# Left sums kept in scratch and built over the operands, and a new order of products in the two-level pairs of a one-core tanh(a @ b + bias)

## The chip, the cores and the metric

The kernel runs on one core of one Trainium2 chip. The metric is the time of one execution on the device in microseconds (us); several executions of the same kernel are timed and their median is given. The engines named below are TensorE (matrix products), VectorE (elementwise sums, transposes), ScalarE (tanh, copies), GpSimd and SyncE (in this kernel both mostly start transfers between DRAM and the core's memory; each works off its own list in order).

## The reference

```
a: 4096 x 4096 float32, b: 4096 x 4096 float32, bias: 4096 float32
out = tanh(a @ b + bias)          # 4096 x 4096 float32
```

## The kernel before, in words

**One level of saving.** The output is worked on in 4 chunks of 1024 columns (`c`), and in each chunk in 16 pairs of two 128-row blocks. Such an item is a 2 x 2 arrangement of blocks: `a11`, `a12`, `a21`, `a22` are the item's four quadrants of a (two row blocks by two halves of the inner dimension; each 128 x 2048 numbers in fp16, already transposed), and `b11` to `b22` are the quadrants of the chunk's b. Instead of eight products of quadrants the kernel computes seven, in the manner of Strassen and Winograd, from sums of quadrants (`PRODUCTS`, L36): m2 = s2 b11, m5 = s5 b22, m3 = a11 d3, m1 = s1 d1, m4 = a22 d4, m6 = s6 e6, m7 = s7 e7. The left sums belong to one item: s2 = a21 - a22, s5 = a12 - a11, s1 = a22 - a11, s6 = a21 - a11, s7 = a22 - a12. The right sums (d1, d3, d4, e6, e7) belong to the chunk. Each of the seven products is 16 matmuls of 128 x 128 by 128 x 512, added up in PSUM (`product` L456, matmul L469); its result is combined with others on VectorE, goes through tanh on ScalarE and is stored (`result` L491, `store` L483, `after` L496). Every sum on VectorE is one `tensor_tensor` (`tt`, L145 and 146).

**Where a quadrant comes from.** In chunk 0 and in the first items of chunk 1 ("natural" items) rows of a are loaded by GpSimd (`load_nat` L226), transposed on VectorE (`turn` L278) and stored once by SyncE into a scratch copy in DRAM (`keep` L298). Later items fetch the four quadrants from scratch on SyncE's queue (`fetch` L303). The quadrants' tiles come two deep (`quads`, bufs=2), the output tiles `o` three deep (`outs`, bufs=3), two small pools (`sums`, bufs=2, and `spare`) hold left sums, and `asum` (L320) makes a left sum from two quadrants: s6 in a21's place and s7 in a12's place, the others in a tile of `sums` or `spare`.

**Order.** The work is laid out by hand in slots, seven per item; `at_slot` (L1431) puts a call into a slot and `prepare` (L1434) places an item's loads, transposes, stores or fetches, and its sums. In each slot the calls are issued in list order, then the products of that slot. Each engine executes its own part of this list in order.

**A second level.** In chunks 1 to 3 two neighbouring items (`p` and `q`) also share products: m3 and m4 of the two (in some pairs m6) are computed together as seven half-size products of eight 256-wide matmuls each instead of two whole ones (`twice` L651, `twice_left` L634 for the left halves `h`, or `twice_four` L923). In chunks 2 and 3, after four and two such items (`FOURS`, L84), the slot list ends and `turn_over` (L1308) leads into a stage of pairs in which four of the seven products are split in this way: `four` (L997), which runs four pairs in chunk 2 and six in chunk 3. In it

- m4, m2, m3 and one or both of m5 and m6 are split. `group0` (L894), `group1` (L900) and `single` (L913) issue the seven half-size products, `multiply` (L874, matmul L885) each one of them; `left` (L848) makes the half-size left sums v1 to v4, each 128 x 1024, in one of four `h` tiles; `copy` and `third` (L889 to L904) move partial results on ScalarE, and the small sums of 128 x 256 join them on VectorE;
- m1 and m7 (and in the last pair of a chunk that is followed by another also m6) stay whole (`whole` L942, matmul L946);
- the right-hand forms t1 to t4 and blocks for m2 and m6 stream in from DRAM on GpSimd's queue (`pull_four` L810, load L816), each as soon as a tile is let go (`let_go` L818, and `hand_back` L829 for tiles that first hold a left sum); those for m3 and m4 stay; those for m5 are made by VectorE in the first pair at the steps given in `M5_AT` (L83, `m5_forms` L972);
- `seed` (L977) zeroes a half of a PSUM bank on ScalarE, `between` (L866) names the half bank for a split product's second partial sum, `four_sum` (L951) makes the left sums, and `give_back` (L980) with `BACK` (L92) fetches the next chunk's operands near the end of chunk 2.

Before, a pair runs m4 beside m2, then m3 beside m6 (or m5), m1 of q, m5 (or m6) with the two halves of m1 of p in between, and m7 of p and q. The last results of a pair are put off into the next one (`left_over`, `more` L992, called four times with an even share).

Of the kernel before, what the change touches and what calls it, by code (L numbers as in the profile page):

```python
# [8 lines left out]
P = 128  # L9
# [72 lines left out]
AHEAD = (), ("a22", "a21", "a11")  # L82
M5_AT = {"t1": -2, "t3": 1, "t2": 3, "t4": 7}  # L83
# [11 lines left out]
    ("b11", 0): 12, ("e6", 0): 2, ("e6", 1): 8, ("m5", "t3"): 13,  # L95
# [10 lines left out]
QUADS = ("a11", "a12", "a21", "a22")  # L106

# [8 lines left out]
def kernel(  # L116
# [203 lines left out]
    def asum(n, name, half=None):  # L320
        s = aset[n]
        x, y = {
            "s2": ("a21", "a22"), "s5": ("a12", "a11"), "s1": ("a22", "a11"),
            "s6": ("a21", "a11"), "s7": ("a22", "a12"),
        }[name]
        over = {"s6": "a21", "s7": "a12"}.get(name)
        if half == 1:
            pass
        elif name == "s6" and n in partner and by_two(n, "m6"):
            s[name] = side[:, :, ds(NB, NB)].rearrange("p a (b m) -> p a b m", m=P)  # L330
            tt(s[name], by_four(s[x]), by_four(s[y]), SUB)
            return
        elif over is None or stays(n):
            s[name] = new_sum([P, T, P], fp16, name, n)
        else:
            s[name] = s[over]
        ts_ = ds(0, T) if half is None else ds(half * TP, TP)
        tt(s[name][:, ts_], s[x][:, ts_], s[y][:, ts_], SUB)
# [295 lines left out]
    def twice_left(n, what, name):  # L634
        left = TWO[what][0]
        p, q = (
            [by_four(aset[i][left])[:, ds(h * TP // TB, TP // TB)] for h in range(2)]
            for i in (n, partner[n])
        )
        x, y = {  # L640
            "s2": (q[0], q[1]), "s5": (p[1], p[0]), "s1": (q[1], p[0]),
            "s6": (q[0], p[0]), "s7": (p[1], q[1]),
        }[name]
        tt(by_four(lefts[PLACE[what][name]]), x, y, SUB)
# [163 lines left out]
    free, held, placed, left_count, homes, wanted, reserved = [], {}, {}, [0], {}, [], []  # L808
# [9 lines left out]
    def let_go(n, what, name):  # L818
        tag = held.pop((what, name))
        c = items[n][0]  # L820
        if wanted and wanted.pop(0):
            reserved.append(tag)
        elif c < NC - 1 and not queue and tag != "sum":
            bring_block(c, tag[:-2], int(tag[-1]))
        else:
            free.append(tag)
        pull_four()

    def hand_back(c):  # L829
        if reserved:  # L830
            tag = reserved.pop(0)
            if c < NC - 1 and tag != "sum":
                bring_block(c, tag[:-2], int(tag[-1]))
            else:
                free.append(tag)
                pull_four()
# [29 lines left out]
    def between(n, what):  # L866
        if n not in fours:
            return bank(n, 0, "w")[:, HALF[TWO[what][3]]]
        i, where, half = {
            "m2": (n, "c", 0), "m4": (n + 1, "c", 1), "m3": (n, "w", 0),  # L870
        }.get(what, (n + 1, "w", 1) if homes.get(what) == "d" else (n, "c", 0))
        return bank(i, 0, where)[:, HALF[half]]

    def multiply(n, what, to, left_, right):  # L874
# [11 lines left out]
        if what in ("m2", "m6"):  # L886
            let_go(n, what, right)
# [63 lines left out]
    def four_sum(n, name, there):  # L951
        x, y = {
            "s2": ("a21", "a22"), "s5": ("a12", "a11"), "s1": ("a22", "a11"),
            "s6": ("a21", "a11"), "s7": ("a22", "a12"),
        }[name]
        st = aset[n]
        if there in QUADS:
            st[name] = st[there]
        elif there in "AB":
            st[name] = side[:, :, ds(NB * "AB".index(there), NB)].rearrange("p a (b m) -> p a b m", m=P)  # L960
        else:
            pool = {"wide": wide, "sum": sums, "spare": spare}.get(there, bops)
            st[name] = pool.tile([P, T, P], fp16, name=name, tag="sum" if there == "spare" else there)
        tt(by_four(st[name]), by_four(st[x]), by_four(st[y]), SUB)

# [26 lines left out]
    def more(calls):  # L992
        for f in left_over[:-(-len(left_over) // calls)]:
            f()
            left_over.pop(0)

    def four(n):  # L997
# [4 lines left out]
        x, y = ("m5", "m6") if last or leave else ("m6", "m5")  # L1002
        mine = {x: "d", y: "w"}
        homes.update(mine)
        pair = {i: items[i][1][0] for i in (p, q)}
        st = {i: state.setdefault((i, 0), {}) for i in (p, q)}
        home = {
            ("s6", p): "a21", ("s6", q): "a21", ("s1", q): "A",
            ("s5", p): "B", ("s1", p): "a11", ("s5", q): "a11", ("s7", p): "a12", ("s7", q): "a12",
        }  # L1010
        if last or leave:
            wanted.extend([1, 0, 1])
        if leave:
            home.update({
                ("s1", p): "A", ("s1", q): "sum",
                ("s6", p): "wide", ("s6", q): "wide", ("s7", p): "wide",
            })

        def make(name, i):
            four_sum(i, name, home[name, i])  # L1020

# [8 lines left out]
        def one_whole(what, i):  # L1030
            _, left_, right = next(v for v in PRODUCTS.values() if v[0] == what)
            whole(i, left_, right, ((bank(i, 0, mine.get(what, "z")), ds(0, NB)),), what in mine)

        def end(name, i, r, j):
            if name == "ds":
                result(st[i][name], pair[i], r, c, j)
            else:
                nc.scalar.activation(st[i][name], st[i][name], TANH)
                store(st[i][name], pair[i], r, c, j)

        def take(what, i, later=False):
            to = bank(i, 0, mine[what])
            if what == "m6":
                tt(st[i]["o"], st[i]["o"], to, ADD)
                ready = ("o", i, 1, 1)
            else:
                tt(st[i]["ds"], st[i]["ds"], to, SUB)
                tt(st[i]["s"], to, st[i]["s"], ADD)
                ready = ("s", i, 0, 1)
            if later:  # L1050
                left_over.append(lambda: end(*ready))
            else:
                end(*ready)
# [5 lines left out]
        def take_d(i):  # L1059
            st[i]["ds"] = temps.tile([P, NB], fp32, name="ds", tag="ds")  # L1060
            tt(st[i]["ds"], bank(i, 0, "d"), bias_bc[:, :NB], ADD)

        def take_z(i):
            st[i]["o"] = new_out()
            tt(st[i]["o"], st[i]["s"], bank(i, 0, "z"), SUB)
# [4 lines left out]
        more(4)  # L1070
        group0(n, "m2")
        left(n, "m2", "v2")
        left(n, "m4", "v3")
        if first:
            make("s6", q)
        more(3)
        step(1)
        w, w2 = group1(n, "m4")
        left(n, "m4", "v4")
        w()  # L1080
        left(n, "m2", "v3")
        if last or leave:
            home["s5", p] = "spare" if reserved[0] == "sum" else reserved[0]
            make("s5", p)
        elif not first:
            make("s6", p)
        more(2)
        u, u2 = group1(n, "m2")
        left(n, "m2", "v4")
        more(1)  # L1090
# [3 lines left out]
        if first:  # L1094
            forms_at(1)
        single(n, "m2", 7)
        u()
        seed(p, "c", 0)
        seed(p, "w", 0)
        seed(q, "w", 1)  # L1100
        left(n, "m3", "v1")
        single(n, "m4", 3, 4)
        step(5)
        u2()
        take_d(p)
        single(n, "m2", 3)
        if last or leave:
            home["s5", q] = "spare" if reserved[1] == "sum" else reserved[1]
            make("s5", q)
        elif not first:  # L1110
            make("s6", q)
        step(6)
        seed(p, "d", 0)
        forms_at(2)
        left(n, x, "v1")
        take_d(q)
        group0(n, "m3")
        left(n, "m3", "v2")
        single(n, "m2", 4)
        step(7)  # L1120
        forms_at(3)
        group0(n, x)
        step(8)
        left(n, x, "v2")
        left(n, "m3", "v3")
        forms_at(4)
        for i in (p, q):
            tt(st[i]["ds"], st[i]["ds"], bank(i, 0, "z"), ADD)
        w, w2 = group1(n, "m3")
        step(9)  # L1130
        left(n, "m3", "v4")
        w()
        left(n, x, "v3")
        for i in (p, q):
            result(st[i]["ds"], pair[i], 1, c, 0)
        if not leave:
            make("s1", q)
            forms_at(5)
            seed(p, "w", 0)
        u, u2 = group1(n, x)  # L1140
        left(n, x, "v4")
        forms_at(6)
        hand_back(c)
        if leave:
            make("s1", p)
        single(n, "m3", 7)
        w2()
        if leave:
            make("s6", p)
            fetch(m, "a21")  # L1150
            make("s7", p)
            fetch(m, "a22")
            fetch(m, "a11")
            fetch(m, "a12")
        single(n, x, 7)
        single(n, "m3", 3, 4)
        step(11)
        if leave:
            one_whole("m1", p)
# [749 lines left out]
```

## Time and profile before

| | |
|---|---|
| median of 3 runs | 1522.07 us (1521.95 to 1522.07) |
| span of the one profiled execution | 1520.0 us, that is 2.07 below the median; no other time of that execution is given |
| bytes moved | 384.58 MB, mean 253 GB/s |
| transfers of a<-scratch (SyncE) | 140 of 512 KB, median 5.4 us from issue to landing |
| transfers of out_dram<-o (SyncE) | 222 of 256 KB, 5.1 us |
| loads of form<-form_m (GpSimd) | 133 of 512 KB, 6.5 us |

The span runs from the first to the last instruction of the core. The profile gives for each engine its busy time and its share of the span; TensorE's weight loads (PEld) run beside its matmuls. A row of the timeline reads: start in us, busy us, engine, line, operation, written<-read tiles, their sizes, how many alike in a row, and in brackets the idle time before with what ended it. Tiles carry the names of the program: `a` is a quadrant or a sum in its place, `s` a left sum (or, at 128 x 512, a partial result), `h` a half-size left sum, `ps` a PSUM bank, `ds` a partial result, `o` an output tile, `form` a right-hand form. A row of the view of stretches reads: start and end, length, then busy us (and instructions) of TensorE, weight loads, VectorE, ScalarE and GpSimd, the granted TensorE clock, the busy share of the DMA engines and GB/s. A row of the transfers reads: queue, written<-read, how many, first to last issue, and under it the time from issue to landing. The time of a fetched transfer counts from its issue in its queue, so a wait for another transfer ahead of it lies before the issue.

### The profile page before, as it was taken

What the parts mean: (1) busy time and instruction counts of PE and PEld (TensorE: products, weight loads), DVE (VectorE), ACT (ScalarE), POOL (GpSimd) and SP (SyncE); (2) the same over time, 40 slices, a digit from 0 to 9 for tenths busy, and PEclk for the clock granted to TensorE, in tenths of its full rate; (3) what the DMA queues carried; (4) which work ended last, traced back from release to release, by engine and by line L of the source; (5) the groups of instructions that cost most, each with busy time, mean ns of one, the idle gap of its engine ahead of it and who ended that gap; (6) DMA issues with size and microseconds to landing.
All of it is one profiled execution on the core that took longest, in us unless ns stands there. A gap on an engine that the chain in (4) does not pass through costs nothing.

```text
span 1520.0 us, 23293 instructions
## 1 busy us (share of the span) xinstructions
PE 1514.8 (100%) x8805; PEld 860.0 (57%) x8805; DVE 1213.7 (80%) x1617; ACT 357.8 (24%) x760; POOL 479.2 (32%) x868
## 2 busy tenths in 40 slices
PE   9999999999999999999999999999999999999999
PEld 4444444444445566544444557777744457777776
DVE  6789877777987777677798777888769969888887
ACT  4432111111221122111122212222212312223222
POOL 8775543333603231344460222111122211111110
PEclk9999999999999999999999999999999999999999
DMA  9999998999979998999995889888966789888874
GB/s 186 180 211 258 280 239 217 225 215 229 190 212 292 267 280 269 231 260 237 228 187 159 292 280 318 307 296 315 320 234 195 226 269 341 317 307 303 304 286 160
DMA packets 203029, 384.58 MB, mean 253 GB/s; under 512 B 25122, under 2 KB 100130, under 8 KB 202916
## 3 DMA queue, kind: packets, MB, share of 16 engines
q0 software_dynamic: 117232, 198.50, 56.4%
q1 hardware_dynamic: 85012, 184.26, 34.9%
q8 instruction: 69, 1.13, 0.3%
q10 hardware_dynamic: 672, 0.33, 0.1%
q14 instruction: 44, 0.36, 0.1%
HBM read 329.78 MB, written 138.94 MB: 308 GB/s over the span
## 4 chain that ended last, share of the span: by engine, by line
PE 99%; DVE 0%; DMA 0%; POOL 0%; issue 0%; ACT 0%; POOLq 0%; DVEq 0%
PE ps L469 58%; PE ps L885 22%; PE ps L946 10%; PE ps L1539 5%; PE ps L667 4%; DMA side<-in_b_dram 0%; DVE h L146 0%; DVE a L146 0%; POOL side L1628 0%; POOL first L1608 0%; DVE form L146 0%; DVE o L146 0%; POOL ident L1615 0%; ACT ds L1266 0%; POOLq L1615 0%
## 5 line engine op out<-in xcount | busy, mean ns | idle before, releaser
L469 PEld LDWEIGHTS <-s 128*128 128x128 f16 x2160 | 211.4, 98 | 249.1 <-DVE s L146 0.2
L469 PEld LDWEIGHTS <-a 128*128 128x128 f16 x1920 | 187.9, 98 | 223.3
L469 PE MATMUL ps<-b,s 128*128 128x512 f16 x1148 | 262.0, 379 | 0.0
L469 PE MATMUL ps<-e,a 128*128 128x512 f16 x908 | 206.9, 379 | 0.0
L469 PE MATMUL ps<-d,a 128*128 128x512 f16 x896 | 202.5, 379 | 0.0
L146 DVE TENSOR_TENSOR s<-a,a 128x2048 f16<-128x2048 f16 (+1 forms) x148 | 178.2, 1207 | 12.7 <-DMA a<-scratch 11.5
L885 PEld LDWEIGHTS <-h 128*128 128x128 f16 x1760 | 171.9, 98 | 26.3 <-DVE h L146 0.4
L271 DVE STREAM_TRANSPOSE a<-nat 128x1024 f16<-128x1024 f16 (+2 forms) x202 | 175.2, 912 | 9.8 <-PE ps L469 8.3
L816 POOL DMA_DIRECT2D form<-form_m x133 | 70.7, 532 | 347.3 <-PE ps L885 318.2
L469 PE MATMUL ps<-d,s 128*128 128x512 f16 x656 | 148.3, 379 | 0.0
L146 DVE TENSOR_TENSOR a<-a,a 128x2048 f16<-128x2048 f16 x120 | 146.0, 1217 | 0.0
L243 POOL DMA_DIRECT2D nat<-in_a_dram x176 | 93.4, 535 | 132.9 <-DVE a L271 58.2
L372 POOL DMA_DIRECT2D b<-in_b_dram x192 | 103.8, 546 | 83.7 <-DVE a L271 31.0
L885 PE MATMUL ps<-form,h 128*128 128x256 f16 x768 | 99.4, 273 | 0.1
L146 DVE TENSOR_TENSOR ps<-ps,x 128x256 f32<-128x256 f32 x128 | 54.0, 429 | 56.4 <-ACT x L891 46.1
L885 PEld LDWEIGHTS <-a 128*128 128x128 f16 x904 | 88.5, 98 | 16.6
L493 ACT ACTIVATE o<-ps 128x512 f32<-128x512 f32 x90 | 54.0, 600 | 158.6 <-issue 94.4
L946 PEld LDWEIGHTS <-a 128*128 128x128 f16 x464 | 44.8, 98 | 44.6
L946 PE MATMUL ps<-e,a 128*128 128x512 f16 (+2 forms) x320 | 68.8, 368 | 0.0
L567 ACT ACTIVATE o<-o 128x512 f32<-128x512 f32 x37 | 23.3, 630 | 175.0 <-DVE o L146 175.0
L146 DVE TENSOR_TENSOR ds<-ds,ps 128x512 f32<-128x512 f32 x75 | 50.2, 683 | 13.6 <-PE ps L946 9.3
L146 DVE TENSOR_TENSOR o<-ds,ps 128x512 f32<-128x512 f32 x40 | 27.4, 685 | 41.2 <-issue 28.9
(190 smaller groups left out, 2001.0 us busy)
## 6 DMA issues: line engine op xcount, KB each, us to landing
a<-scratch SPq DMA_DIRECT2D x140, 512.0 KB, 5.4
form<-form_m POOLq DMA_DIRECT2D x133, 512.0 KB, 6.5
out_dram<-o SPq DMA_DIRECT2D x222, 256.0 KB, 5.1
nat<-in_a_dram POOLq DMA_DIRECT2D x288, 128.0 KB, 7.2
scratch<-a SPq DMA_DIRECT2D x48, 512.0 KB, 6.7
b<-in_b_dram POOLq DMA_DIRECT2D x160, 128.0 KB, 5.5
scratch<-a SPq DMA_DIRECT2D x32, 256.0 KB, 5.7
cast<-in_b_dram POOLq DMA_DIRECT2D x64, 128.0 KB, 9.2
```

The lines of the kernel that those rows point to most:

```text
L146: nc.vector.tensor_tensor(out=out_, in0=in0, in1=in1, op=op)
L243: nc.gpsimd.dma_start(out=tl[ds(q * QP, QP), :, :], in_=src.rearrange("(mb p) k -> p mb k", p=QP),)
L271: nc.vector.transpose(dst[:, ds(b0 * tb, n * tb), :].rearrange("P (b t) (mb p) -> P mb b t p", t=tb, p=QP), src[:, :, ds(b0, n), :].rearra ...
L372: nc.gpsimd.dma_start(out=dst[ds(q * QP, QP), ds(t, nt)], in_=src)
L469: nc.tensor.matmul(st[where], at, bt, start=(what == "m2" or n < LEAD and what == "m1") and i == 0, stop=i == len(ts_) - 1, skip_group_che ...
L493: nc.scalar.activation(o, src, TANH)
L567: nc.scalar.activation(o, o, TANH)
L667: nc.tensor.matmul(to, at, bt, start=False, stop=t == TP - 1, skip_group_check=True)
L816: nc.gpsimd.dma_start(out=rights[what, name], in_=forms[what, name])
L885: nc.tensor.matmul(to, at, bt, start=False, stop=t == TP - 1, skip_group_check=True)
L946: nc.tensor.matmul(to[:, half], at[:, t // TB, t % TB], bop[right, t // TB][:, t % TB, half], start=anew and t == 0, stop=t == T - 1, skip ...
L1539: nc.tensor.matmul(mb[m % 4, j], aq[m, kt // T][:, kt % T, :], right(kt, j), start=fresh and kt == k0, stop=stop and kt == k1 - 1, skip_gr ...
```

## The change: what it does

- `asum` follows a table `SUMS`. s2 is made over a21 and s5 over a12. Natural items make them and then store them, so that scratch holds s2 and s5 in the places of a21 and a12; a11 and a22 are still stored right after their transpose. An item that fetches from scratch gets s2 and s5 ready-made and makes neither. s6 is s2 + s1 and s7 is s1 - s5; in the two-level stage s1 is made over a11. s6 moves by two slots and s7 by one in some items. `twice_left` takes its halves by a table.
- `four_sum`, `hand_back` and the lists around it go. A tile of a form is let go by the product that used it, without further holding.
- `four` runs in a new order: m4 beside m3, m2 beside m5, m1 of p, m6 split (or whole, in the pair that leaves a chunk) with m1 of q among it, and m7 of p and q. So m5 is split in all pairs, and m2's and m5's results of both items are finished next to each other. `between` names other half banks. `left_over` holds one call, run at once in the next pair. Seeds, fetches and sums are placed anew around it.
- `turn_over` has fetches, sums and seeds in new places, and fetches a12 of the stage's first two items there, right behind the m7 of p and of q; `after` (L563 and L564) has started a fetch of the same quadrant with each of these m7.
- The constants `M5_AT`, `AHEAD` and `BACK` change with it.

The built program has 8805 matmuls before and after, 1365 two-input operations on VectorE before and 1279 after, 514 and 518 transfers by SyncE.

```diff
-AHEAD = (), ("a22", "a21", "a11")
-M5_AT = {"t1": -2, "t3": 1, "t2": 3, "t4": 7}
+AHEAD = (), ("a21", "a11")
+M5_AT = {"t1": -2, "t3": 1, "t2": 2, "t4": 3}
...
-    ("b11", 0): 12, ("e6", 0): 2, ("e6", 1): 8, ("m5", "t3"): 13,
+    ("b11", 0): 6, ("e6", 0): 2, ("e6", 1): 10, ("m5", "t3"): 12,
...
+SUMS = {
+    "s2": ("a21", "a22", SUB), "s5": ("a12", "a11", SUB), "s1": ("a22", "a11", SUB),
+    "s6": ("s2", "s1", ADD), "s7": ("s1", "s5", SUB),
+}
...
     def asum(n, name, half=None):
         s = aset[n]
-        x, y = {...}[name]
-        over = {"s6": "a21", "s7": "a12"}.get(name)
+        over = {"s2": "a21", "s5": "a12", "s6": "a21", "s7": "a12"}.get(name)
+        if name == "s1" and n in fours:
+            over = "a11"
+        if name in ("s2", "s5"):
+            s[name] = s[over]
+            if not natural(n):
+                return
...
+        x, y, op = SUMS[name]
...
-        tt(s[name][:, ts_], s[x][:, ts_], s[y][:, ts_], SUB)
+        tt(s[name][:, ts_], s[x][:, ts_], s[y][:, ts_], op)
...
     def between(n, what):
...
-            "m2": (n, "c", 0), "m4": (n + 1, "c", 1), "m3": (n, "w", 0),
-        }.get(what, (n + 1, "w", 1) if homes.get(what) == "d" else (n, "c", 0))
+            "m4": (n, "w", 0), "m3": (n + 1, "w", 0), "m2": (n, "w", 1), "m5": (n + 1, "w", 1),
+            "m6": (n, "c", 0),
+        }[what]
...
     def four(n):            # the new order, its main line (not the leaving or last pair)
         step(0)
         group0(n, "m4")
         left(n, "m4", "v2")
-        more(4)
-        group0(n, "m2")
-        left(n, "m2", "v2")
+        more()
+        group0(n, "m3")
+        left(n, "m3", "v2")
         left(n, "m4", "v3")
...
+        u, u2 = group1(n, "m3")
         step(2)
         single(n, "m4", 7)
         w2()
+        left(n, "m3", "v4")
         u()
+        single(n, "m3", 7)
+        u2()
+        forms_at(1)
...
         single(n, "m4", 3, 4)
         step(5)
+        for i in (p, q):
+            asum(i, "s2")
+            asum(i, "s5")
+        left(n, "m2", "v1")
+        take_d(p)
+        seed(p, "d", 0)
+        single(n, "m3", 3)
+        take_d(q)
+        left(n, "m5", "v1")
+        forms_at(2)
+        group0(n, "m2")
+        left(n, "m2", "v2")
+        take_c(p)
+        single(n, "m3", 4)
+        step(6)
+        left(n, "m5", "v2")
+        take_c(q)
+        seed(p, "c", 0)
+        group0(n, "m5")
+        step(7)
+        left(n, "m2", "v3")
+        forms_at(3)
+        w, w2 = group1(n, "m2")
+        left(n, "m5", "v3")
+        w()
+        asum(p, "s1")
+        if not last:
+            fetch(m, "a22")
+        left(n, "m2", "v4")
+        u, u2 = group1(n, "m5")
+        step(8)
+        single(n, "m2", 7)
+        forms_at(4)
+        w2()
+        left(n, "m5", "v4")
+        u()
+        single(n, "m5", 7)
+        asum(p, "s6")
+        u2()
+        seed(p, "w", 0)
+        single(n, "m2", 3, 4)
+        step(9)
+        take_m2(p)
+        asum(p, "s7")
+        single(n, "m5", 3)
+        asum(q, "s1")
...
+        take_m2(q)
+        asum(q, "s6")
+        if not leave:
+            left(n, "m6", "v1")
+        take_m5(p)
+        single(n, "m5", 4)
+        step(10)
+        one_whole("m1", p)
+        take_m5(q)
+        asum(q, "s7")
...
+        left(n, "m6", "v2")
+        group0(n, "m6")
+        take_m1(p)
+        left(n, "m6", "v3")
+        one_whole("m1", q)
+        w, w2 = group1(n, "m6")
+        left(n, "m6", "v4")
+        w()
+        take_m1(q)
...
+        one_whole("m7", p)
...
+        single(n, "m6", 7)
+        w2()
+        single(n, "m6", 3)
+        take_m7(p)
+        single(n, "m6", 4)
+        take_m6(p)
...
     def turn_over(c):
...
-        aset[q]["s6"] = side[:, :, ds(0, NB)].rearrange("p a (b m) -> p a b m", m=P)
-        tt(aset[q]["s6"], by_four(aset[q]["a21"]), by_four(aset[q]["a11"]), SUB)
         asum(q, "s1")
-        asum(q, "s7")
-        fetch(m, "a22")
-        fetch(m + 1, "a21")
+        asum(q, "s6")
+        fetch(m, "a11")
...
+        fetch(m, "a12")
         left(m, "m4", "v1")
+        left(m, "m3", "v1")
...
         product(q, *PRODUCTS[10])
+        fetch(m + 1, "a12")
...
-                if n:
+                if n and name in ("a11", "a22"):
                     at_slot(at[1], keep, n, name)
...
-        sums_at["s6"] = 12 if late else 13 if end_ else 8
+        sums_at["s6"] = 12 if late else 13 if end_ else 10
...
         for name, at in sums_at.items():
             at_slot(s0 + at, asum, n, name)
+            if natural(n) and name in ("s2", "s5"):
+                at_slot(s0 + at, keep, n, "a21" if name == "s2" else "a12")
```

More of the change, by code (lines that the diff above doesn't have):

```diff
@@ L816, in pull_four, with let_go @@
             nc.gpsimd.dma_start(out=rights[what, name], in_=forms[what, name])
-    def let_go(n, what, name):
+    def let_go(what, name):
         tag = held.pop((what, name))
[L820 to L824, printed above, removed]
+        if returned and not queue and tag != "sum":
+            bring_block(returned[0], tag[:-2], int(tag[-1]))
         else:
@@ L949, in whole @@
                 )
[L951 to L964, printed above, removed]
     def m5_form(name):
@@ L1001, in four @@
         leave = m not in fours and not last
-        x, y = ("m5", "m6") if last or leave else ("m6", "m5")
-        mine = {x: "d", y: "w"}
-        homes.update(mine)
+        homes.update({"m5": "d", "m6": "w"})
         pair = {i: items[i][1][0] for i in (p, q)}
         st = {i: state.setdefault((i, 0), {}) for i in (p, q)}
[L1007 to L1020, printed above, removed]
         def forms_at(k):
@@ L1069, in four @@
         left(n, "m4", "v2")
[L1070 to L1072 removed]
+        more()
+        group0(n, "m3")
+        left(n, "m3", "v2")
         left(n, "m4", "v3")
[L1074 to L1076 removed]
         step(1)
         w, w2 = group1(n, "m4")
+        left(n, "m3", "v3")
+        w()
         left(n, "m4", "v4")
[L1080 to L1090, printed above, removed]
+        u, u2 = group1(n, "m3")
         step(2)
@@ L1093, in four @@
         w2()
-        if first:
-            forms_at(1)
-        single(n, "m2", 7)
-        u()
-        seed(p, "c", 0)
-        seed(p, "w", 0)
+        left(n, "m3", "v4")
+        u()
+        single(n, "m3", 7)
+        u2()
+        forms_at(1)
+        seed(p, "z", 0)
+        seed(p, "w", 1)
         seed(q, "w", 1)
-        left(n, "m3", "v1")
         single(n, "m4", 3, 4)
         step(5)
-        u2()
[L1105 to L1111, printed above, removed]
```

302 lines of the change are left out of this document (92 added, 210 removed).

## The prediction

> **What bounds the kernel now.** I read the profile's page first, then who waited for whom on TensorE, the busy time by stages, the chain of work that ended last, and VectorE's timeline at one place. The page:
>
> ```profile
> span 1520.0 us, 23293 instructions
> PE 1514.8 (100%) x8805; PEld 860.0 (57%) x8805; DVE 1213.7 (80%) x1617; ACT 357.8 (24%) x760; POOL 479.2 (32%) x868
> PEclk9999999999999999999999999999999999999999
> PE 99%; DVE 0%; DMA 0%; POOL 0%; issue 0%; ACT 0%; POOLq 0%; DVEq 0%
> ```
>
> TensorE is busy for 1514.8 of 1520.0 us at full clock, and 99% of the chain is its own work. Its waits are listed in full by the view of waits for TensorE:
>
> ```profile
> PE warm L1599 <- DVE idle L407: 1.3, 1, 1.3
> PE tp L1640 <- DVE first L1635: 0.5, 1, 0.5
> PE ps L1539 <- DMA side<-in_b_dram: 0.3, 1, 0.3
> ```
>
> All three lie in the opening, which the change does not touch. The chain in order of time, and the busy times of two stages and of the first pair with its own order of products:
>
> ```profile
> 99.70 359.15 PE ps L469 x1664
> 928.55 22.71 PE ps L885 x208
> 1513.43 3.51 PE ps L946 x32
> ```
>
> ```profile
> 100.00:480.00 380.00, 380.00 (x1790) 175.03 (x1789) 312.09 (x372) 68.89 (x123) 156.01 (x290) 1.00 0.99 231
> 928.00:973.00 45.00, 45.00 (x350) 33.98 (x349) 40.20 (x62) 11.11 (x30) 7.43 (x14) 1.00 0.88 311
> 1250.00:1295.00 45.00, 44.88 (x348) 33.74 (x347) 41.67 (x65) 11.35 (x31) 7.96 (x15) 1.00 0.91 327
> ```
>
> A 512-wide matmul costs 359.15/1664 = 0.216 us, a 256-wide one 22.71/208 = 0.109 us, run after run without a hole. So the kernel is bound by its number of matmuls, and everything else counts only by what it makes TensorE wait. In the third stretch of the last fence TensorE misses 0.12 us of 45: that is all there is to win back. VectorE is the next engine, with 40.2 and 41.7 of 45 us in the first pair of the two-level stage (the columns after the length are TensorE, weight loads, VectorE, ScalarE, GpSimd), against 312 of 380 in the plain stage.
>
> **The change part by part.**
>
> *Matmuls.* The built program has 8805 before and after, 5173 of them 512 wide and 3584 256 wide in both. Cost 0.
>
> *Left sums.* The built program has 298 sums of 128x2048 in place of 384. The groups by line give their price:
>
> ```profile
> L146 DVE TENSOR_TENSOR s<-a,a 128x2048 f16<-128x2048 f16 (+1 forms) x148 | 178.2, 1207 | 12.7 <-DMA a<-scratch 11.5 <-PE ps L469 1.1
> L146 DVE TENSOR_TENSOR a<-a,a 128x2048 f16<-128x2048 f16 x120 | 146.0, 1217 | 0.0
> ```
>
> 86 x 1.22 = 105 us leave VectorE, four per two-level pair (40) and the rest in the other items. No row of TensorE waits for them, so the gain is 0. In the plain stages VectorE keeps its order but for s6 and s7, which move up to two slots later and still stand several products ahead of their use; a21 and a12 are stored after their sum and not after the transpose, on the same queue. TensorE had no wait there and VectorE gets lighter: 0. If that cover were gone, each late sum would cost at most its 1.22 us.
>
> *The two-level pairs, new order.* A pair now runs m4 with m3, m2 with m5, then m1, m6 and m7; there are ten such pairs (four in chunk 2, six in chunk 3). VectorE's queue decides whether its operands are in time. Its pace, from its timeline before:
>
> ```profile
> 929.60 1.22 DVE L146 TENSOR_TENSOR a<-a,a 128x2048 f16<-128x2048 f16 x1
> 930.73 0.69 DVE L146 TENSOR_TENSOR h<-a,h 128x1024 f16<-128x1024 f16 x1
> ...
> 938.32 0.68 DVE L146 TENSOR_TENSOR h<-a 128x1024 f16<-128x1024 f16 x1
> 938.92 0.43 DVE L146 TENSOR_TENSOR ps<-ps,x 128x256 f32<-128x256 f32 x1
> 939.25 0.68 DVE L146 TENSOR_TENSOR ds<-ps,bias_bc 128x512 f32<-128x512 f32 x1
> 939.85 0.68 DVE L146 TENSOR_TENSOR h<-a 128x1024 f16<-128x1024 f16 x1
> ```
>
> The durations overlap; from start to start a 2048 sum takes 1.13, a 1024 sum 0.60, a 512-wide f32 one 0.60, a 256-wide one 0.33. In the *first* pair of each chunk the queue also makes the six halves of m5's forms t3, t2 and t4, and M5_AT now draws t2 and t4 together at steps 2 and 3. From the end of m4's product 7, VectorE has no hole until v1 of m6, which m6's second product needs: 15 halves of 1024 (nine of left sums, six of forms) and v1 itself, six 512-wide, seven 256-wide, and s1, s6, s7 of the first item and s1, s6 of the second. That is 15 x 0.60 + 4 x 1.13 + 6 x 0.60 + 7 x 0.33 = 19.4, s6 in full 1.22 because v1 reads it, v1 in full 0.68, and 0.20 from TensorE to VectorE, as here:
>
> ```profile
> 972.76 1.04 PE L885 MATMUL ps<-d,a 128*128 128x256 f16 x8
> ...
> 972.96 1.41 DVE L146 TENSOR_TENSOR ds<-ds,ps 128x512 f32<-128x512 f32 x2 [0.39 <-PE ps L946]
> ```
>
> (TensorE begins its next product at 972.76; VectorE, which waited for the one before, begins at 972.96.) Together 21.5 us. TensorE meanwhile has 20 products of eight 256-wide matmuls and m1 of the first item: 20 x 0.873 + 16 x 0.216 = 20.9 us. **Late by 0.6 us, in two pairs: 1.2.** The bounds are 0 (a queue that gains 3% on these paces) and 1.7 each (half the six forms' 3.6 us uncovered). In the other eight pairs the forms are gone and the queue is 3 us early: 0.
>
> [...] VectorE's starts above overlap by 0.08 us. [...] What full spacing would do is a rival below.
>
> *Stores.* m2's and m5's results of a pair now take four output tiles from a pool of three, so m5's second result waits until m2's first has landed. ScalarE and the transfers:
>
> ```profile
> 1490.00 0.36 ACT L904 COPY ps<-ps 128x256 f32<-128x256 f32 x1 [2.26 <-PE ps L885]
> 1490.27 0.38 ACT L891 COPY x<-ps 128x256 f32<-128x256 f32 x1
> 1490.54 1.16 ACT L493 ACTIVATE o<-ds 128x512 f32<-128x512 f32 x2
> ```
>
> ```profile
> L484 SPq DMA_DIRECT2D out_dram<-o x21: 332/337/498, 930.4 to 1080.9; - x21
> ...
> DMA to landing us min/median/max: 2.0/4.8/8.2
> ```
>
> ```profile
> L484 SPq DMA_DIRECT2D out_dram<-o x30: 332/337/358, 1284.7 to 1491.7; - x30
> ...
> DMA to landing us min/median/max: 2.5/5.1/7.3
> ```
>
> (The last two are the output's transfers in chunks 2 and 3.) From m2's second product v2 to m6's third, with v2, TensorE has 11 products and m1 of both items: 16.5 us. On the other side stand 0.20 to ScalarE, its two copies 0.27 + 0.38, VectorE up to m2's first result 2 x 1.13 + 2 x 0.60 + 4 x 0.33 = 4.8, that result 0.68, the tanh 0.58, the landing, then m5's result and difference 1.20, s7 1.13, v2 0.68: 9.9, and 0.2 for the two hand-overs between. So the landing may take 6.4 us; queued behind it are v2 to v4 of m6. Median 4.8 to 5.1: usually free. Ends: 0, and 1.8 (8.2 - 6.4) in every pair. I take **one pair in ten late, by half of that: 0.9.**
>
> *Fetches.* SyncE's list grows from 514 to 518 transfers: at the change-over into each two-level stage a12 of both items is fetched twice, and the second fetch waits in SyncE's queue for the first's landing, with the later fetches and stores behind it. The fetch at this place before, in chunk 2 and chunk 3, and GpSimd's form loads around the latter:
>
> ```profile
> L305 SPq DMA_DIRECT2D a<-scratch x1: 327/327/327, 928.6 to 928.6; - x1
> ...
> DMA to landing us min/median/max: 5.9/5.9/5.9
> ```
>
> ```profile
> L305 SPq DMA_DIRECT2D a<-scratch x1: 406/406/406, 1250.4 to 1250.4; - x1
> ...
> DMA to landing us min/median/max: 8.9/8.9/8.9
> ```
>
> ```profile
> 1251.87 0.53 POOL L816 DMA_DIRECT2D form<-form_m  x1 [2.42 <-DMA form_m<-stage]
> 1253.23 0.53 POOL L816 DMA_DIRECT2D form<-form_m  x1 [0.83 <-PE ps L885]
> ```
>
> VectorE needs it for v1 of m5: nine products from the fetch's release (7.9) and 4.6 of its own queue make 12.5 us for two landings. Twice 5.9 is 11.8: free. The loads beside the 8.9 are freed by m2's products, which now come later, so I take 5.9 for both chunks: 0. The ends are 0 (no wait is below nothing) and 2 x 8.9 - 12.5 = 5.3 in one pair. At the end of chunk 2 the next item's a21 likewise follows a store's landing in SyncE's queue; with median landings it is early: 0.
>
> *Sum.* 1520.0 + 1.2 + 0.9 = 1522.1 us of span; the median of the runs, 1522.07, is 2.07 above the profiled span, so **1524.2 us**, 0.14% up. About 0.2% (3 us) is what a measurement of this kernel can tell from no change.
>
> **The rivals.**
>
> *All is hidden.* The queue gains the 0.6 us and no store is late: 1522.1. For it: VectorE loses 105 us in all; against it: the first pair's queue is full from end to end.
>
> *The double fetch decides (slower).* Once two landings take over 12.5 us, every further us moves VectorE's full queue, and TensorE with it. With 8.9 + 5.9 in chunk 3: 2.3, with twice 8.9: 5.3. With the 2.1 above: 1526.5 to 1529.5. Against it: the loads that move away. The opening shows what a long stop could add:
>
> ```profile
> 1.26 3.59 PE L1599 MATMUL warm<-idle 128*128 128x512 f16 x8 [1.26 <-DVE idle L407]
> ```
>
> Eight 512-wide matmuls take 3.59 us there and 1.73 later. [...]
>
> *Stores are late in half of the pairs.* Five times 0.9 instead of one: 1527.8. It decides once the typical landing passes 6.4 us; the medians speak against it, the denser traffic about m2's store (a fetch and three form loads) for it.
>
> *Full spacing on VectorE.* Then the first pair's queue takes 15 x 0.68 + 5 x 1.22 + 6 x 0.68 + 7 x 0.43 + 0.68 + 0.20 = 24.3, 3.4 late twice: 1529.8. [...]
>
> That the sums do not go away is excluded by the built program's count.
>
> **How the numbers follow.** Forecast 0.41; all hidden 0.22; double fetch 0.17; stores 0.15; full spacing 0.04; faster by over 0.2% 0.01, since only 0.12 us can be won. Within 0.2% are the first two: 0.63; slower 0.36. The likeliest case alone spans 1523.3 to 1525.1. The range leaves out full spacing, the upper half of the double fetch and the 0.01: 1521.9 to 1528.0.
>
> **What would show it.** TensorE's waits should name v1 of m6 (h by VectorE) once near 957 and once near 1279 us, 0.6 each; VectorE's sum should fall by about 105 us; its waits for a12 from scratch should be 0 there; single waits for out_dram may appear on o. I am wrong if TensorE waits in every pair, if VectorE stands over 1 us for the second a12, or if any plain stage shows a wait.

## The result, and the profile after

The changed kernel takes **1533.95 us** (median of 4 runs, 1532.82 to 1536.71) against 1522.01 of the kernel before (4 runs, 1521.94 to 1522.07): a ratio of 1.0081, 95% interval 1.0066 to 1.0095. The forecast was 1524.2 with a range up to 1528.0. The profiled execution is the slowest of the four: 1536.71 us, of which 1535.0 are its span.

The page of the changed kernel, the lines that answer to those shown of before:

```profile
span 1535.0 us, 23236 instructions
PE 1521.8 (99%) x8805; PEld 862.0 (56%) x8805; DVE 1120.6 (73%) x1531; ACT 361.3 (24%) x762; POOL 477.6 (31%) x868
...
PE 96%; DMA 3%; DVE 1%; issue 0%; ACT 0%; DVEq 0%; ACTq 0%
```

VectorE has lost 93 us of work, as many matmuls are run as before, and yet 3% of the chain is now a transfer. TensorE's waits after the opening (us in total, times, longest), from the view of waits:

```profile
PE ps L879 <- DVE h L150: 5.8, 3, 3.2
PE ps L879 <- ACT ps L957: 1.9, 1, 1.9
...
PE ps L879 <- ACT ps L891: 0.2, 1, 0.2
```

The stretches of the prediction, and one of 7 us, with the granted clock as the third number from the right:

```profile
100.00:480.00 380.00, 380.00 (x1791) 174.95 (x1789) 304.97 (x364) 70.27 (x125) 155.53 (x290) 1.00 1.00 231
928.00:973.00 45.00, 41.96 (x319) 30.64 (x318) 34.55 (x55) 10.21 (x28) 6.34 (x12) 1.00 0.83 293
1250.00:1295.00 45.00, 39.78 (x286) 29.12 (x285) 31.01 (x50) 9.95 (x27) 5.93 (x12) 0.92 0.75 271
1277.00:1284.00 7.00, 6.43 (x33) 4.64 (x34) 6.94 (x13) 1.30 (x4) 1.06 (x2) 0.53 0.32 112
```

The plain stage is as full as before. The loss lies in the first pair of both two-level stages, and for some us behind 1277 TensorE runs at half pace. The chain of work that ended last, in order of time, with the transfers in it:

```profile
101.73 359.15 PE ps L475 x1664
...
930.58 2.50 PE ps L879 x23
933.08 9.00 DMA a<-scratch
...
942.09 4.19 DMA a<-scratch
...
1261.40 10.58 DMA a<-scratch
...
1272.00 4.81 DMA a<-scratch
```

Two landings stand one behind the other, twice: the second fetch of the second item's a12 is issued at 942.09, when the first, issued at 933.08, has landed (933.08 + 9.00). SyncE's queue at this place shows what held the first one:

```profile
931.70 0.32 SPq L309 DMA_DIRECT2D a<-scratch  x1
932.11 0.38 SPq L490 DMA_DIRECT2D out_dram<-o  x1
932.60 0.87 SPq L309 DMA_DIRECT2D a<-scratch  x2
933.56 0.46 SPq L490 DMA_DIRECT2D out_dram<-o  x1
942.09 12.79 SPq L309 DMA_DIRECT2D a<-scratch  x2
```

The row at 931.70 is the second fetch of the *first* item's a12, which waited for its own first; a store, the next a21 and the second item's first fetch come only then. VectorE and TensorE at both places, and at the change-over of chunk 3, from the timeline:

```profile
946.31 0.69 DVE L150 TENSOR_TENSOR h<-a 128x1024 f16<-128x1024 f16 x1 [3.15 <-DMA a<-scratch]
947.06 1.05 PE L879 MATMUL ps<-form,h 128*128 128x256 f16 x8 [1.63 <-DVE h L150]
...
1256.76 1.29 DVE L150 TENSOR_TENSOR stage<-e,stage 128x1024 f16<-128x1024 f16 x2 [9.53 <-DMA form_m<-stage]
1258.69 0.63 ACT L573 ACTIVATE o<-o 128x512 f32<-128x512 f32 x1 [13.76 <-DVE o L150]
1259.22 0.66 ACT L957 CAST ps<-zeros 128x256 f32<-128x256 f16 x2
1259.64 1.03 PE L879 MATMUL ps<-g,h 128*128 128x256 f16 x8 [1.91 <-ACT ps L957]
...
1276.83 0.69 DVE L150 TENSOR_TENSOR h<-a 128x1024 f16<-128x1024 f16 x1 [4.09 <-DMA a<-scratch]
1277.57 1.89 PE L879 MATMUL ps<-form,h 128*128 128x256 f16 x8 [3.19 <-DVE h L150]
```

m5's v1 (`h<-a`) waits for a12, and TensorE for v1. The rows at 1256 to 1259 are a second, separate loss: VectorE stands 9.5 us for the stage, a tile of a form whose store to DRAM has to land before it is written again; behind it stands m7's result of p, behind that the tanh in ScalarE's queue, behind that the seeds of the PSUM halves, and for these TensorE waits. In the kernel before the same wait was

```profile
1246.27 1.29 DVE L146 TENSOR_TENSOR stage<-e,stage 128x1024 f16<-128x1024 f16 x2 [4.45 <-DMA form_m<-stage]
```

and TensorE did not feel it.

Where the 15.0 us between the two spans lie, counted as what is between the starts of successive matmuls beyond their pace (0.216 and 0.109 us):

| place | us |
|---|---|
| opening (first 12 us) | 2.0 |
| change-over and first pair of chunk 2 | 4.0 |
| chunk 2 behind it, late stores | 0.5 |
| change-over of chunk 3, late seeds | 2.5 |
| first pair of chunk 3: stops | 3.6 |
| the same: matmuls at half pace after the stop | 2.9 |
| less before's own 0.3, and an end that is 0.25 shorter | -0.5 |

The terms are rounded. The 2.0 of the opening are not the change's: the same work stands there in both kernels, but in this execution TensorE stayed at half pace until about 10.4 us, while the traces of before and of e1 to e4 show full pace from their rows at 5.34 to 5.62 us on (0.25 or 0.26 us to the start of the row behind, here 0.41). One such row, first before, then after:

```profile
5.34 0.41 PE L1640 MATMUL tp<-ident,first 128*128 128x128 f16 x4 [0.49 <-DVE first L1635]
```

```profile
5.60 0.62 PE L1552 MATMUL tp<-ident,first 128*128 128x128 f16 x4 [0.74 <-DVE first L1547]
```

Runs of the kernel before in the later comparisons spread from 1521.4 to 1524.2 us, so single executions of it can be 2 us longer too.

### The profile page after: what moved, and what is told of

It is laid out like the page before. It is cut to its first block, busy times and chain, and to the rows that moved or that the text cites. A ratio compares the mean times of both kernels' runs of the same rounds, so it can differ in the third digit from the quotient of the medians.

```text
span 1535.0 us, 23236 instructions
## 1 busy us (share of the span) xinstructions
PE 1521.8 (99%) x8805; PEld 862.0 (56%) x8805; DVE 1120.6 (73%) x1531; ACT 361.3 (24%) x762; POOL 477.6 (31%) x868
## 3 DMA queue, kind: packets, MB, share of 16 engines
q8 instruction: 69, 1.13, 0.3%
## 4 chain that ended last, share of the span: by engine, by line
PE 96%; DMA 3%; DVE 1%; issue 0%; ACT 0%; DVEq 0%; ACTq 0%
PE ps L475 58%; PE ps L879 19%; PE ps L940 9%; PE ps L1451 5%; PE ps L672 4%; DMA a<-scratch 2%; DMA out_dram<-o 0%; DVE h L150 0%; DVE a L150 0%; DMA coarse<-in_a_dram 0%; PE warm L1511 0%; DVE form L150 0%; PE tp L1552 0%; DVE ps L150 0%; PE spread L438 0%
## 5 line engine op out<-in xcount | busy, mean ns | idle before, releaser
L475 PEld LDWEIGHTS <-a 128*128 128x128 f16 x3264 | 319.3, 98 | 378.7 <-DMA a<-scratch 0.4
L475 PE MATMUL ps<-b,a 128*128 128x512 f16 x1148 | 262.0, 379 | 0.0
L475 PE MATMUL ps<-e,a 128*128 128x512 f16 x932 | 212.1, 379 | 0.0
L475 PE MATMUL ps<-d,a 128*128 128x512 f16 x896 | 202.5, 379 | 0.0
L879 PEld LDWEIGHTS <-a 128*128 128x128 f16 x1320 | 129.8, 98 | 24.7 <-issue 0.8
L475 PEld LDWEIGHTS <-s 128*128 128x128 f16 x848 | 83.0, 98 | 97.7
L150 DVE TENSOR_TENSOR a<-a,a 128x2048 f16<-128x2048 f16 (+1 forms) x97 | 115.8, 1203 | 0.2
L940 PEld LDWEIGHTS <-a 128*128 128x128 f16 x688 | 66.7, 98 | 70.9 <-issue 0.3
L940 PE MATMUL ps<-e,a 128*128 128x512 f16 (+2 forms) x360 | 77.7, 370 | 0.0
L150 DVE TENSOR_TENSOR h<-a,h 128x1024 f16<-128x1024 f16 x110 | 75.2, 685 | 0.0
L475 PE MATMUL ps<-side,a 128*128 128x512 f16 x288 | 73.9, 379 | 0.0
L940 PE MATMUL ps<-d,a 128*128 128x512 f16 x320 | 72.2, 379 | 0.0
L879 PE MATMUL ps<-form,a 128*128 128x256 f16 x536 | 70.3, 275 | 0.0
```

Of the source, the lines that this page charges most:

```text
L150: nc.vector.tensor_tensor(out=out_, in0=in0, in1=in1, op=op)
L475: nc.tensor.matmul(st[where], at, bt, start=(what == "m2" or n < LEAD and what == "m1") and i == 0, stop=i == len(ts_) - 1, skip_group_che ...
L879: nc.tensor.matmul(to, at, bt, start=False, stop=t == TP - 1, skip_group_check=True)
L940: nc.tensor.matmul(to[:, half], at[:, t // TB, t % TB], bop[right, t // TB][:, t % TB, half], start=anew and t == 0, stop=t == T - 1, skip ...
```

## The experiments

Each run is compared with the kernel before on the same chip; the medians of before were 1522.2 to 1522.6. "e1" and so on are the names used below.

**e1, single fetches.** The edit, in `turn_over`:

```diff
         seed(m + 1, "w", 0)
-        fetch(m, "a12")
         left(m, "m4", "v1")
...
         product(q, *PRODUCTS[10])
-        fetch(m + 1, "a12")
```

> The changed kernel without the two second fetches of a12 at the change-over into the two-level stages. Theory A (the second fetch waits in SyncE's queue for the landing of the first, and VectorE for both): the two stops of TensorE before m5's v1 go, 4.0 us in chunk 2 and 6.4 us in chunk 3 (3.2 of stop and 3.2 of slow clock behind it); the 2.1 us near 1257 and the 0.5 us after late stores stay. 1522.0 + 2.6 = 1524.6 us, between 1523.5 and 1526. Theory B (the new order needs a12 too early even for one landing): TensorE still stops there, 1529 or more.

Measured: 1526.04 us (9 runs), ratio 1.0026 (1.0016 to 1.0035). Theory A holds for the size: 7.9 us are gone. TensorE's waits that are left, in the time of chunks 2 and 3:

```profile
PE ps L879 <- ACT ps L957: 1.0, 1, 1.0
PE ps L879 <- DVE h L150: 0.7, 2, 0.4
PE ps L475 <- DMA a<-scratch: 0.5, 1, 0.5
PE ps L475 <- DVE s L150: 0.2, 1, 0.2
```

The `h` in the second row is m2's v4, once in each first pair, and with two smaller gaps each pair loses 0.75 us (0.52 + 0.11 + 0.12). The late seeds cost 1.55, the leaving of chunk 2 0.95. Together 4.0; the medians differ by 3.8. The median is 0.04 above the range that was expected, since theory A had not counted the first pairs.

**e2, three fetches.** `fetch(m, "a12")` and `fetch(m + 1, "a12")` stand twice in `turn_over`.

> The changed kernel with a12 of both items fetched three times at each change-over. Theory A (landings one behind the other): one more landing of 4.2 to 4.8 us in each of the two stages, and a longer slow clock in chunk 2, whose stops get as long as that of chunk 3: 1534 + 9 + 3 = 1546 us, between 1542 and 1549. Theory C (the added bytes slow the other transfers, not the order): two more transfers of 512 KB at some 400 GB/s are 2.6 us: 1535 to 1537.

Measured: 1553.68 us (5 runs), ratio 1.0205 (1.0191 to 1.0219). The direction is A's and C falls, but A was sized too small: two more landings per stage went into the queue, not one, for the first item's fetches stand ahead of the second's. (For the rate that C takes, 400 GB/s: the changed kernel's trace has 411 from 924.0 to 934.5.) TensorE's waits for left sums; two of them in chunk 2, with the matmuls behind each; and the stretches behind the last stop of each chunk:

```profile
PE ps L879 <- DVE h L150: 22.3, 4, 7.7
```

```profile
944.00 1.05 PE L879 MATMUL ps<-form,h 128*128 128x256 f16 x8 [2.77 <-DVE h L150]
...
954.52 1.89 PE L879 MATMUL ps<-form,h 128*128 128x256 f16 x8 [7.74 <-DVE h L150]
```

```profile
954.50:961.00 6.50, 6.48 (x35) 4.77 (x36) 6.43 (x12) 1.30 (x4) 1.06 (x2) 0.57 0.22 60
1295.60:1302.00 6.40, 6.40 (x33) 4.69 (x34) 6.33 (x12) 1.30 (x4) 1.06 (x2) 0.55 0.16 55
```

**e3, the second fetches sent elsewhere.**

```diff
-        fetch(m, "a12")
+        nc.sync.dma_start(out=dram.tile([P, T, P], fp16, name=name), in_=there)
```

(`there` is the scratch of the same a12, and likewise for `m + 1`.)

> The changed kernel with the two second fetches sent to tensors of their own in DRAM that nobody reads: the same bytes read at the same places of SyncE's queue, but nothing that has to land first. Theory A: as with the second fetches gone, 1524.6 us (1523.5 to 1527). Theory C (the bytes): as the changed kernel, 1532 to 1535.

Measured: 1527.11 us (6 runs), ratio 1.0030 (1.0018 to 1.0041). The same bytes without the wait cost 1.1 us over e1, which lies within the spread of the two runs, and with the wait 7.9. The order in SyncE's queue is the cause; the traffic is a small part of it at most. What the bytes do can be seen in chunk 3: the fetch of the second item's a21 lands late there, and VectorE stands 1.0 us for it at 1266.

**e4, the second fetches in the kernel before.** `fetch(m, "a12")` behind m7 of p and `fetch(m + 1, "a12")` behind m7 of q, added to before's `turn_over`.

> The kernel before with the same two second fetches of a12 put behind m7 of p and of q at each change-over. There a12 is first read well behind m2, m4 and m6 of the first pair. Theory A (the wait counts because the new order reads a12 some 20 us earlier): no stop, 1522.0 to 1522.8 us. Theory D (a second fetch costs by itself, whoever reads it, because the fetches and stores behind it in the queue start later): 1526 or more.

Measured: 1522.92 us (11 runs), ratio 1.0005 (0.9996 to 1.0014): no change that can be told. TensorE's only waits in chunks 2 and 3 were

```profile
PE ps L885 <- DMA form<-form_m: 1.0, 2, 0.8
```

and none for a12. (The kernel before has no such waits for form loads in these chunks; the median does not show them.) The doubling is harmless where a12 is read late; it takes the new order, with m5 as the fourth product, to make it cost.

**e11 and e12, one doubling alone.** The changed kernel without the second fetch of the second item (e11), and without that of the first (e12).

> The changed kernel with only the first item's a12 fetched twice, the second item's once. Theory J (neither doubling alone uses up the 12.5 us; in the changed kernel the first item's second fetch held the second item's first one back by 2.5 to 4.5 us, and that with two landings was too much): the second item's single fetch starts near 933.1 and lands 9.0 us later, 1.1 us ahead of VectorE's need near 943.2; in chunk 3 near 1272.0 against 1272.7. No stop there, 1526.0 us, between 1525.3 and 1527. Rival K (the two landings of the second item alone decide, as the prediction had it): the same time, since they are gone. This run tells only whether the hold-back alone costs.

> The changed kernel with only the second item's a12 fetched twice, the first item's once. Theory J: the first fetch starts near 928.7 as in e1, lands by 937.2, and the second one lands 4.2 to 5 us later, ahead of the need near 943; in chunk 3 255.9 + 9.2 + 4.8 is 1269.9 (counted from 1000), just ahead of 1270.4. No stop or one of under 1 us, 1526 to 1527 us. Rival K: two landings alone are 13.2 us (9.0 + 4.2) and 15.4 us (10.6 + 4.8) against 12.5, stops of 0.7 and 2.9 us, 1529.5 us.

Measured: e11 1527.09 us (7 runs), ratio 1.0030 (1.0019 to 1.0040); e12 1529.49 us (5 runs), ratio 1.0045 (1.0031 to 1.0058). Over e1 that is 1.1 and 3.5 (0.7 and 3.1 when each is taken against its own kernel before); both together were 7.9, more than the sum. The 1.1 of e11 lies within the spread of the two runs, and its median is 0.09 above the range that was expected. VectorE's waits for fetches in the first pair of chunk 3, in e11 and in e12:

```profile
1265.44 0.69 DVE L150 TENSOR_TENSOR h<-a 128x1024 f16<-128x1024 f16 x1 [1.22 <-DMA a<-scratch]
```

```profile
1270.19 0.69 DVE L150 TENSOR_TENSOR h<-a 128x1024 f16<-128x1024 f16 x1 [3.55 <-DMA a<-scratch]
```

In chunk 2 neither kernel loses more than 0.15 us over e1's first pair: there theory J is right, and only the hold-back and the two landings together use up the slack. In chunk 3 e11's row is m2's v1, which waits for the second item's a21; m5's v1 follows at 1267.25 without a wait. So the hold-back alone makes a12 late in neither chunk. The same wait for a21 stands in e3 (1.0 us) and in e5 below (1.2 us), where nothing is held back. e12's row is m5's v1 and does wait for a12: two landings alone stop TensorE for 2.2 us (theory K). By SyncE's list the first fetch of the second item's a12 stands there behind m7's store of p, and that store waits for the result which the stage holds up on VectorE.

**e5 and e6, the late seeds.** Both start from e1. e5 moves `fetch(m, "a21")` behind `product(p, *PRODUCTS[10])`; e6 is

```diff
-        asum(q, "s7")
         slot(9)
         slot(10)
+        asum(q, "s7")
```

> The kernel with single fetches (e1) and, in the change-over, the fetch of the first item's a21 moved from ahead of m7 of p to behind it. In e1 GpSimd's store of the stage took 9.2 us to land at the change-over of chunk 3 (7.3 in the kernel before), with five fetches issued within 5 us of it; VectorE stood 8.6 us for it and TensorE lost 1.55 us behind that. Theory E (the fetch moved beside this store is what makes it late): landing 7.3 to 7.8, the loss at most 0.3 us, 1524.6 us. Theory F (the store is issued later, because s7 stands ahead of the stage's sum on VectorE; the traffic is nothing new): landing 9, loss as before, 1526.0 us.

> The kernel with single fetches (e1) and, in the change-over, q's s7 made behind the stage's sum and not ahead of it (1.13 us on VectorE). Theory F: the stage's sum and its store start 1.1 us earlier, and the loss of 1.55 us falls to 0.4 or 0.5: 1524.9 us. Theory E: the store lands at the same time as in e1, since the transfers beside it decide: 1526.0 us, loss 1.4 or more.

Measured: e5 1526.90 us (6 runs), ratio 1.0031 (1.0019 to 1.0043); e6 1525.02 us (11 runs), ratio 1.0017 (1.0008 to 1.0026). The stage's wait in e1, e5 and e6:

```profile
1251.25 1.29 DVE L150 TENSOR_TENSOR stage<-e,stage 128x1024 f16<-128x1024 f16 x2 [8.61 <-DMA form_m<-stage]
```

```profile
1250.83 1.29 DVE L150 TENSOR_TENSOR stage<-e,stage 128x1024 f16<-128x1024 f16 x2 [8.52 <-DMA form_m<-stage]
```

```profile
1249.21 1.30 DVE L150 TENSOR_TENSOR stage<-e,stage 128x1024 f16<-128x1024 f16 x2 [5.73 <-DMA form_m<-stage]
```

Theory E falls: without a21 beside it the store still took 9.1 us, and the later fetch of a21 goes with another late left sum (VectorE then waits 1.2 us at 1265 for the second item's a21). Theory F is right about the cause and too small in its size: with s7 behind the stage's sum the store lands in 7.4 us and not in 9.2. It is issued at 1241.69 and not at 1241.98, though VectorE's sums ahead of it run 0.85 us later (1238.92 against 1238.07), so 1.1 us earlier against the work around it, and the loss goes from 1.55 to nothing.

**e7 and e8, m5's forms in the first pair.** Both start from e1, with one constant each:

```diff
-M5_AT = {"t1": -2, "t3": 1, "t2": 2, "t4": 3}
+M5_AT = {"t1": -2, "t3": 1, "t2": 2, "t4": 4}    # e7
+M5_AT = {"t1": -2, "t3": -1, "t2": 2, "t4": 3}   # e8
```

> The kernel with single fetches (e1) and m5's form t4 one step later (behind m2's v4 on VectorE). In e1 TensorE lost 0.52 us for m2's v4 and 0.12 for m6's v1 in each first pair, 0.64 together; the prediction had 0.6, all at m6's v1. Theory G (VectorE's queue as a whole is 0.6 us too long up to m6's v1, and the place of a form only decides which left sum shows it): 0.5 to 0.7 us per first pair, now for m5's v4 or m6's v1; time as e1, 1526.0 us. Theory H (it is only t4's place ahead of m2's v4): under 0.2 us per first pair, 1525.0 us.

> The kernel with single fetches (e1) and m5's form t3 made at the end of the change-over and not within the first pair: 1.2 us less in VectorE's queue of the first pair. Theory G: no stop for m2's v4 or m6's v1 in either first pair, 1.3 us less than e1, 1524.7 us. Theory H: t4 stays ahead of m2's v4, the stops stay: 1526.0 us. Against both: t3's two halves could make the first pair's first left sums late by up to 1.2 us each time, 1527.

Measured: e7 1526.07 us (9 runs), ratio 1.0024 (1.0015 to 1.0034); e8 1524.63 us (11 runs), ratio 1.0017 (1.0008 to 1.0026). In e7 the stops did not go, they moved to VectorE's small sums (the `ps` in brackets):

```profile
953.16 1.03 PE L879 MATMUL ps<-form,a 128*128 128x256 f16 x8 [0.43 <-DVE ps L150]
```

0.99 us per first pair, against e1's 0.75. In e8 they are gone (two small gaps of 0.2 together are left in one of the two), and 1.4 us with them. Theory G holds, though e7's stops are longer than the 0.5 to 0.7 that it gave: VectorE's queue as a whole was too long. TensorE's waits in chunks 2 and 3 of e8:

```profile
PE ps L879 <- ACT ps L957: 1.1, 1, 1.1
PE ps L940 <- DVE s L150: 0.6, 1, 0.6
PE ps L879 <- DVE h L150: 0.3, 1, 0.3
```

**e9 and e10, the repairs together.** e9 is e6 with e8's constant. e10 moreover puts `take_m5(q)` behind `left(n, "m6", "v2")` (in the leaving pair behind `asum(q, "s7")`).

> The kernel with single fetches (e1), q's s7 behind the stage's sum and m5's form t3 at the end of the change-over: the two repairs together. Theory (the three losses are separate and add up): from e1's 3.8 us go 1.55 at the change-over of chunk 3 and 1.4 in the two first pairs; left is what late stores cost, 0.5 to 1 us: 1522.2 + 0.9 = 1523.1 us, between 1522.5 and 1524. Rival (the repairs use the same slack): one of the two stops comes back, 1524.5 or more.

> As the run before it, and m5's result of q, which takes the fourth output tile, stands behind m6's v2 (in the pair that leaves the chunk behind s7) in VectorE's queue and not ahead of them. Theory (a late store is felt only because v2 and s7 stand behind the instruction that waits for the output tile): the stops of 0.4 to 0.5 us near 1052 and 1097 go, 1522.4 us, within 0.1% of the kernel before. Rival (v3 and the results of m1 are next in line and wait as long): the stops move by a product, 1523.1 us.

Measured: e9 1522.98 us (11 runs), ratio 1.0002 (0.9993 to 1.0011); e10 1522.74 us (11 runs), ratio 1.0001 (0.9992 to 1.0010). TensorE's waits in chunks 2 and 3, e9 first:

```profile
PE ps L879 <- DVE h L150: 0.3, 1, 0.3
```

```profile
PE ps L475 <- DMA a<-scratch: 0.2, 1, 0.2
```

The losses were separate and add up: with each run taken against its own kernel before, e6 is 1.3 us better than e1, e8 1.7 and e9 3.0. With the stops mended the new order takes the time of the old one. e10's last repair cannot be told from e9 by the time. In its trace TensorE waits for no late store in any pair, but in e9's it does so only once, for 0.3, so this one execution does not settle what the move is worth. A fourth output tile, the direct test, was not tried.

## Why the prediction was wrong, point by point

- **What bounds the kernel:** right. TensorE has nothing to win, and with the stops mended (e9) the time is that of before, with 94 us less on VectorE.
- **Matmuls, 0:** right.
- **Left sums, gain 0 and no cost:** right for the plain stages (380.00 of 380 busy). VectorE lost 93 us, not 105; from start to start, at 1.13, the 86 sums are 97. Wrong at the change-over of chunk 3: s7 of q now stands right ahead of the stage's sum (before, VectorE made it 7 us ahead of that sum, at 1230.30 against 1237.32), and this made the seeds late, 1.55 us in e1 and 2.5 in the profiled run. The step "VectorE gets lighter: 0" looked at the sums and not at what is queued behind each of them.
- **First pair, 0.6 us late in each chunk:** right in size, 0.75 in e1, and by the mechanism named (e7, e8). The first and largest stop is at m2's v4, some 8 us ahead of m6's v1; the sum had been made for the end of the queue alone. (Its upper bound, half of 3.6, is 1.8 and not 1.7; nothing hangs on it.) The rival of full spacing on VectorE, 3.4 us per pair, falls by the same number.
- **Stores, one pair in ten, 0.9:** about right. In the changed kernel, e1 and e5 to e8, late stores cost 0 to 0.5 us in all ordinary pairs together, and stores and fetches 0.2 to 0.95 at the leaving of chunk 2.
- **Fetches, 0:** this is **the step that failed**: without the second fetches (e1) the time is 1526.04, inside the range. It had the mechanism, and the slack of 12.5 us was right: in the profiled run VectorE was ready for a12 at 943.16 (946.31 - 3.15), and q's m7, which frees the tile of a12, ended at 930.58, 12.6 us earlier. On the other side it put two landings of 5.9. Measured were 2.5 us in which the first item's second fetch held the queue (to 933.08), 9.00 and 4.19: 15.7. Two things were wrong. The 5.9 was one row, and the row of 8.9 beside it was argued away because form loads would move; with single fetches (e1) the second item's a12 still took 8.5 us in chunk 2 and 9.2 in chunk 3, the figures that e12's expectation took from e1's trace. And the wait was counted for the second item only, though the text says that the later fetches stand behind the second fetch of each. In chunk 3 the same chain met SyncE's queue late, behind the stage: the first fetch was issued at 1261.40, VectorE was ready for a12 11.3 us later (1276.83 - 4.09), and the two landings took 10.58 and 4.81. The sign that the prediction had named, VectorE standing over 1 us for the second a12, came in both chunks (3.15 and 4.09).
- **The rival of the double fetch**, chance 0.17: the right mechanism, at 2.3 to 5.3 us in one pair instead of 7.9 in both. The half pace behind the longer stop, which is not in its 1526.5 to 1529.5, cost 2.9 more (granted clock 0.53 from 1277 to 1284).

The trace shows these waits in SyncE's queue itself: over 900 to 1120 us its fetches waited three times for a fetch from scratch, 14.3 us together. The second fetches are issued at 931.70 and 942.09, when the first ones have landed, and the a21 and a12 that stand behind the one of 931.70 go out only after it, from 932.60 on.

## What to carry to other kernels

A transfer that overwrites the target of one still in flight cost little here by its bytes (1.1 us in e3, within the spread), but a full landing in its issuing queue (4.19 and 4.81 us for the second item's), for itself and for all behind it; before a product is moved ahead, look for every such pair in the queue that feeds it. Where a budget is compared with a landing time, take the slow rows of the busiest stretch, and count every wait in the queue ahead of the transfer, not only its own. When a sum gets a new place in an in-order queue, ask for each instruction that now stands right behind it who waits for that one's result, across engines: here a sum of 1.13 us delayed a store, a tanh and a seed.

## What the runs showed of the hardware that was not expected

- **Behind the longer stops TensorE went on at half pace.** After stops of 1.63 us in the changed kernel and 2.77 us in e2 (start to start 3.05) the matmuls went on at full pace; after 3.19 us (3.45 start to start) the granted clock was 0.53 over 7 us and cost 2.9 us more, and after 7.74 us in e2 0.57 over 6.5 us. Half pace lasted about 6.0 us behind the stop of 3.19 (from 1277.57 to 1283.5). In these runs the step lies between 2.8 and 3.2 us of waiting; each is a single stop, and that the length alone decides is not shown.
- **The losses in one in-order queue did not simply add.** The two doubled fetches cost 1.1 and 3.5 us alone and 7.9 together, 2.9 of it by the slow clock behind the longer stop.
- A store of 512 KB took 9.2 us among fetches (e1) and 7.4 us when it was issued 1.1 us earlier against the work around it (e6).
